# The head of a hybrid mLSTM / differential-attention layer: first modulation weights, then tokens, then the rest

## The chip, the cores and the metric

The kernel runs on one core of one Trainium2 chip. The metric is the device time of one execution in microseconds (us); of the kernel before, three timed executions are shown (median 2418.31 us, 2416.95 to 2418.4), and one more was profiled. The engines are named as in the profile: PE is TensorE (PEld its weight loads), DVE VectorE, ACT ScalarE, POOL GpSimd, SP SyncE, which issues DMAs.

## What is computed

One layer over 256 latent tokens `x` and 256 context tokens `ctx`, 2048 channels, all in float32. Only the beginning matters here:

```python
mod = jax.nn.silu(c) @ w_mod[l] + b_mod[l]            # sh1, sc1, ... for latent tokens
mod_c = jax.nn.silu(c_ctx) @ w_mod[l] + b_mod[l]      # csh1, csc1, ... for context tokens
h = modulate(rmsnorm(x, norm1_w[l]), sh1, sc1)
hc = modulate(rmsnorm(ctx, norm1_w[l]), csh1, csc1)
y, yc = token_mixer(h, hc, ...)                       # begins with h @ w_in and hc @ w_in
```

Then come the mLSTM and attention branches, the merge, and an expert retrieval (PEER).

## The kernel before, in words

The stretch around the change is called the head here: everything in `build` from line 308 to `drain()` on line 439. It makes the modulated, transposed tokens `hL` and `hC` (128 channels on the partitions, 16 chunks of channels) and, as they come, multiplies them with the first two blocks of `w_in` ("vm" and "zm").

**Modulation weights.** The main loop (line 408) goes over the 16 chunks k. Each chunk has four loads of 512 KB on SP's queue (line 417, through `load`, line 102) into a ring of 11 buffers. Every load is used by four matmuls (line 419), which the trace records as 8 each. The sums of a chunk stand in one PSUM tile `m`; `mod_evac` copies it (line 355), adds four partial sums with small matmuls (line 359) and writes shift and scale `mc` (lines 362, 364).

**Tokens.** `tokens()` loads four tiles of 128 tokens (1024 KB each, line 329), squares each on ACT for the norm (line 333), takes the power -1/2 on POOL (line 188), scales the tile on DVE (line 336), and turns it by 16 PE transposes in four groups (line 341), each group copied from a PSUM tile `m` back over the tile by ACT or DVE (line 343).

**h.** `h_chunk(k)` reads chunk k of all four turned tiles, applies shift and scale on ACT (line 377), rounds on DVE (line 381) and takes the remainder on POOL (line 382). A gate matmul (line 368) follows for each chunk. `vm_part` and `zm_part` are the products with `w_in` (line 264): a vm part has 24 matmuls of 512 columns, a zm part 12, and there are 8 of each. A `w_in` piece is loaded (line 104), rounded to `hi` on ACT (line 120) and its remainder `lo` made on DVE (line 123).

**Order.** The steps are generators in a queue `back`; `pump(n)`, called after each load of a chunk, runs n of them. So `pump` sets the order in the program. The order in which each engine then gets its instructions is made at build time by a list scheduler: it follows the program, but takes a later instruction whose inputs it believes to be ready when an engine would otherwise stand idle. At run time each engine goes through its list in that order.

**PSUM.** The pool of `m` tiles has four buffers. One is held by the gate sums `g_ps` through the head, two by `zm_acc` from the first zm part on; the sums of a chunk, their second step and the groups of transposes share what is left.

**POOL's queue** loads small tables at the start: the gate weights `gwp` (832 KB, line 322), `gbias`, `iota`, `bic` (lines 324 to 326) and two bias rows spread over all partitions (`brow`, 256 KB each, lines 346 and 347, through `row_to_all`, line 154). `crow` (line 411) is a small load that stands in the program at chunk 4.

Of the kernel before, what the change touches and what calls it, by code (L numbers as in the profile page):

```python
# [30 lines left out]
P = 128  # L31
# [42 lines left out]
def build(tc, a, dump=None):  # L74
    nc = tc.nc
# [18 lines left out]
    def col(shape, name, src=None, dt=F32):  # L94
        t = cst.tile(shape, dt, name=name)
        if src is not None:
            nc.gpsimd.dma_start(t, src)
        return t
# [3 lines left out]
    def load(src, pool, bufs, queue=nc.sync):  # L102
        r = pool.tile([P, 1024], F32, name="raw", tag="raw", bufs=bufs)
        d = queue.dma_start(r, src)  # L104
        if by_four[0]:
            tc.keep_in_program_order(d)
        return r
# [45 lines left out]
    def row_to_all(dst, src, n):  # L153
        nc.gpsimd.dma_start(dst, bass.AP(tensor=src.tensor, offset=src.offset, ap=[[0, P], [1, n]]))
# [6 lines left out]
    ident = col([P, P], "ident")  # L161
# [10 lines left out]
    iota = col([P, P], "iota")  # L172
    bic = col([P, 64], "bic")
# [10 lines left out]
    def rstd(pool, ss, n, w, name):  # L184
        v = pool.tile([P, w], F32, name=name + "v", bufs=1)
        nc.vector.tensor_scalar(v, ss, 1.0 / n, EPS, op0=OP.mult, op1=OP.add)
        r = pool.tile([P, w], F32, name=name, bufs=1)
        nc.gpsimd.tensor_tensor(r, v, mhalf[:, :w], op=OP.pow)  # L188
        return r
# [4 lines left out]
    def acc_tile():  # L194
        return psA.tile([P, 512], F32, name="acc", tag="acc")

    def m_tile():
        return psM.tile([P, 512], F32, name="m", tag="m")
# [7 lines left out]
    def brow_tile(row, blk):  # L206
        b = gco.tile([P, 512], F32, name="brow", tag="brow", bufs=2)
        row_to_all(b, a["b_in_rows"][row, blk * 512:(blk + 1) * 512], 512)
        return b
# [6 lines left out]
    def hT(s, c, k, tok=None):  # L216
        t = (hC if c else hL)[s][k // 4][:, k % 4]
        return t if tok is None else t[:, tok * P:(tok + 1) * P]
# [4 lines left out]
    back = []  # L223
# [6 lines left out]
    def step(q):  # L230
        while q:
            try:
                next(q[0])
                return
            except StopIteration:
                q.pop(0)

    def pump(rate, ahead=2, beside=0):
        for i, (q, r) in enumerate(((front, ahead), (back, rate), (side, beside))):
            credit[i] += r if q else 0  # L240
            while credit[i] > 0.99:
                credit[i] -= 1
                step(q)
# [75 lines left out]
    xt = [x4[:, i, :] for i in range(4)]  # L319
    sq = st.tile([P, D], mybir.dt.bfloat16, name="sq")  # L320
    gwp = st.tile([P, KT, 104], F32, name="gwp")
    nc.gpsimd.dma_start(gwp, a["w_gate"])
    gbias = cst.tile([104, 1], F32, name="gbias")
    nc.gpsimd.dma_start(gbias, a["gate_bias"])
    nc.gpsimd.dma_start(iota, a["iota"])
    nc.gpsimd.dma_start(bic, a["b_in_cols"])
    def tokens():
        for i in range(4):
            nc.sync.dma_start(xt[i], (a["x"] if i < 2 else a["ctx"])[(i % 2) * P:(i % 2 + 1) * P, :])
            yield  # L330
        for i in range(4):
            ss = st.tile([P, 1], F32, name=f"ss{i}")
            nc.scalar.activation(sq, xt[i], AF.Square, accum_out=ss)
            yield
            rs = rstd(st, ss, D, 1, f"rs{i}")
            nc.vector.tensor_scalar(xt[i], xt[i], rs, None, op0=OP.mult)
            yield
            for j in range(4):
                tp = m_tile()
                for k in range(4):  # L340
                    nc.tensor.transpose(tp[:, k * P:(k + 1) * P], xt[i][:, (4 * j + k) * P:(4 * j + k + 1) * P], ident)
                d = xt[i][:, j * 512:(j + 1) * 512]
                (nc.vector.tensor_copy if j % 2 else nc.scalar.copy)(d, tp)
                yield

    vm_brow = brow_tile(1, 0)
    zm_brow = brow_tile(2, 0)
    vm_acc = [acc_tile() for _ in range(4)]
    g_ps = m_tile()
    mod1 = {}  # L350
# [2 lines left out]
    def mod_evac(k, ps):  # L353
        r4 = st.tile([P, T], F32, name="r4", tag="r4", bufs=2)
        nc.vector.tensor_copy(r4, ps[:, 0:T])
        yield
        pc = m_tile()
        for s in range(2):
            mm(pc[:, 2 * s:2 * s + 2], lhsT=r4[:, s * P:(s + 1) * P], rhs=sel4, start=True, stop=True)
        m = mod1[k]  # L360
        for s in range(2):
            nc.vector.tensor_scalar(m[:, s, :], pc[:, 2 * s:2 * s + 2], b1c[:, s, k:k + 1], float(s),
                                    op0=OP.add, op1=OP.add)
        nc.vector.tensor_scalar(m[:, 1, :], m[:, 1, :], nwc[:, 0, k:k + 1], None, op0=OP.mult)
        yield

    def gate_part(k, hf):
        mm(g_ps[0:104, :], lhsT=gwp[:, k, :], rhs=hf, start=k == 0, stop=k == 15)
# [3 lines left out]
    def h_chunk(k):  # L372
        mc = mod1[k]
        hf = st.tile([P, 512], F32, name="hf", tag="hf", bufs=2)
        for c in range(2):
            w = slice(c * T, (c + 1) * T)
            nc.scalar.activation(hf[:, w].rearrange("p (i t) -> p i t", i=2), x4[:, 2 * c:2 * c + 2, k * P:(k + 1) * P],
                                 AF.Identity, bias=mc[:, 0, c:c + 1], scale=mc[:, 1, c:c + 1])
        for c in range(2):
            w = slice(c * T, (c + 1) * T)  # L380
            nc.vector.tensor_copy(hT(0, c, k), hf[:, w])
            nc.gpsimd.tensor_tensor(hT(1, c, k), hf[:, w], hT(0, c, k).bitcast(F32), op=OP.subtract)
        hfs.append(hf)
        yield
        if k:
            gate_part(k - 1, hfs[k - 1])
        if k == KT - 1:
            yield
            gate_part(k, hf)
        yield  # L390
# [3 lines left out]
    def first_part(j):  # L394
        (vm_part, zm_part)[j % 2](j // 2)
# [4 lines left out]
    def zm_part(kp):  # L400
        if kp == 0:
            zm_acc.extend(m_tile() for _ in range(2))
        token_part(zm_acc, take(), kp, h_lhs, kp == 0, kp == 7)

    back.append(tokens())
    part = 0
    ready = [0]
    for k in range(KT):
        if k == 4:
            crow = st.tile([KT, P], F32, name="crow")  # L410
            nc.gpsimd.dma_start(crow, a["c_row"])
            nc.scalar.activation(crow, crow, AF.Silu)
            nc.gpsimd.dma_start(s_dram.rearrange("o (k p) -> (o k) p", p=P), crow)
        mod1[k] = st.tile([P, 2, 2], F32, name="mc", tag="mc", bufs=4)
        ps = m_tile()
        for kp in range(4):
            w = load(a["w_mod1"][k, kp], stx, MOD_BUFS)
            for k4 in range(4):
                mm(ps[32 * k4:32 * k4 + 32, 0:T], lhsT=s1[:, 4 * kp + k4, :], rhs=w[:, k4 * T:(k4 + 1) * T],
                   start=kp == 0, stop=kp == 3, skip_group_check=True)  # L420
            pump(2 if k < 6 else 1)
            if kp % 2:
                if part // 2 * 2 + 1 < ready[0]:
                    first_part(part)
                    part += 1
                ready[0] = len(hfs)
        g = mod_evac(k, ps)
        next(g)
        front.append(g)
        back.append(h_chunk(k))  # L430
        look[0] = 2
    while part < 16:
        while part // 2 * 2 + 1 >= len(hfs):
# [1273 lines left out]
```

## Time and profile before

| what | value |
|---|---|
| median of three timed executions | 2418.31 us |
| the profiled execution's own time | 2422.88 us |
| its span, first to last instruction | 2421.2 us |
| PE busy over the span | 2326.2 us (96%) |
| DVE, ACT, POOL busy | 64%, 47%, 37% |
| read from HBM | 524.33 MB |
| first matmul of the head | 6.46 us |
| first matmul with `w_in` | 40.06 us |

The busy shares are means over stages with different limits. For a change in the first 40 us of 2421 the views by stretch and by order of time are the ones to read.

### The profile page before, as it was taken

Reading aid. Unit: us, or ns where it says so; the run is one execution under the profiler, and the core shown is the slowest. Engines: PE = TensorE matmul, PEld = TensorE weight load, DVE = VectorE, ACT = ScalarE, POOL = GpSimd, SP = SyncE. Lnnn points to the kernel's source line nnn. Section 1 sums busy time; section 2 is a strip of 40 time slices with the busy share of each in tenths; the row PEclk is TensorE's granted clock in tenths of the full one; section 3 lists DMA queues with packets and bytes.
Section 4 is the critical chain, followed back from the end, with each engine's and each line's share of the span. In section 5 each row is a group of like instructions: output and inputs, shape, how many; then the busy total and the mean of one; then the engine's idle time right before and its main releaser. Section 6 shows DMA issues by size and latency. Waiting matters only on the chain. (4 is left out here: it accounts for less than half of the span.)

```text
span 2421.2 us, 38180 instructions
## 1 busy us (share of the span) xinstructions
PE 2326.2 (96%) x14434; PEld 1971.9 (81%) x14434; DVE 1542.8 (64%) x2808; ACT 1140.5 (47%) x1913; POOL 894.1 (37%) x910
## 2 busy tenths in 40 slices
PE   6999999999999999989999989999999998999996
PEld 3679989998898999779888878887889887665663
DVE  3357874669766768564788976675665545444445
ACT  3231322244548544444446766794358643333333
POOL 2132201236533200000145564672237524656552
PEclk9999999999999999999999999999999999999998
DMA  9969855875536788755565567788765568998884
GB/s 383 347 201 321 318 192 180 287 214 165 153 115 189 239 281 272 244 197 184 165 200 173 174 183 222 218 219 238 216 191 170 163 213 293 385 368 321 344 337 158
DMA packets 235899, 571.04 MB, mean 236 GB/s; under 512 B 85138, under 2 KB 118723, under 8 KB 221248
## 3 DMA queue, kind: packets, MB, share of 16 engines
q1 hardware_dynamic: 153744, 338.29, 43.7%
q0 software_dynamic: 47120, 212.72, 24.7%
q10 hardware_dynamic: 34848, 17.57, 2.5%
q8 instruction: 113, 1.85, 0.3%
q14 instruction: 74, 0.61, 0.1%
HBM read 524.33 MB, written 38.93 MB: 233 GB/s over the span
## 5 line engine op out<-in xcount | busy, mean ns | idle before, releaser
L120 ACT CAST hi<-raw 128x1024 fp32r<-128x1024 f32 x528 | 552.4, 1048 | 794.0 <-PE acc L275 257.3
L123 DVE TENSOR_TENSOR lo<-raw,hi 128x1024 fp32r<-128x1024 f32 x465 | 590.2, 1272 | 328.8 <-ACT hi L120 323.0
L80 PE MATMUL s<-h,hi 128*128 128x512 f32 x2048 | 740.4, 403 | 1.0 <-ACT hi L120 1.0
L80 PE MATMUL s<-h,lo 128*128 128x256 f32 x2048 | 579.5, 283 | 20.8 <-POOL lo L123 11.5
L80 PEld LDWEIGHTS s<-h,hi 128*128 128x128 f32 x2048 | 388.2, 190 | 88.7 <-ACT hi L120 1.7
L275 PE MATMUL acc<-hL,hi 128*128 128x256 f32 x2048 | 420.5, 285 | 0.0
L80 PEld LDWEIGHTS s<-h,lo 128*128 128x128 f32 x2048 | 390.0, 190 | 28.7 <-POOL lo L123 14.2
L275 PEld LDWEIGHTS acc<-hL,hi 128*128 128x128 f32 x2048 | 339.4, 192 | 4.2 <-issue 3.9
L275 PE MATMUL acc<-hL,lo 128*128 128x256 f32 x1024 | 291.3, 285 | 3.9 <-DVE lo L123 3.9
L123 POOL TENSOR_TENSOR lo<-raw,hi 128x1024 fp32r<-128x1024 f32 x63 | 152.4, 2419 | 275.5 <-ACT hi L120 261.7
L1525 PE MATMUL v<-hi,l 128*128 128x512 f32 x704 | 197.7, 398 | 8.7 <-ACT l L1450 8.6
L1444 DVE TENSOR_TENSOR lo<-vraw,hi 128x1024 fp32r<-128x1024 f32 x106 | 129.2, 1234 | 118.1 <-ACT hi L1442 116.3
L275 PEld LDWEIGHTS acc<-hL,lo 128*128 128x128 f32 x1024 | 196.2, 192 | 5.9 <-DVE lo L123 4.9
L104 POOL DMA_DIRECT2D raw<-w_mod x128 | 67.9, 531 | 305.9 <-DVE raw L508 284.7
L508 DVE SCALAR_TENSOR_TENSOR raw<-raw,cr 128x1024 f32<-128x1024 f32 x128 | 154.9, 1221 | 36.9 <-DMA raw<-w_mod 21.4
L1223 POOL TENSOR_SCALAR o<-iota,i1T,gT 128x128 f32<-128x128 f32 x128 | 140.8, 1107 | 94.5 <-PE g L80 50.3
L1442 ACT CAST hi<-vraw 128x1024 fp32r<-128x1024 f32 x106 | 108.7, 1046 | 138.4 <-PE v L1525 134.0
L1525 PEld LDWEIGHTS v<-hi,l 128*128 128x128 f32 x704 | 132.5, 190 | 49.5 <-issue 10.6
L1429 POOL DMA_INDIRECT vraw<-expert_v,idxV x99 | 105.7, 1068 | 105.4 <-DVE l L1451 31.5
L275 PE MATMUL acc<-hC,hi 128*128 128x256 f32 x512 | 134.0, 283 | 0.0
L1507 DVE TENSOR_REDUCE act<-s 128x256 f32<-128x512 f32 x126 | 86.4, 686 | 58.1 <-PE s L80 52.8
L1429 POOL DMA_INDIRECT ag<-ag_dram,idxG x99 | 102.6, 1036 | 47.3 <-issue 26.2
(406 smaller groups left out, 3971.9 us busy)
## 6 DMA issues: line engine op xcount, KB each, us to landing
raw<-expert_u SPq DMA_DIRECT2D x256, 512.0 KB, 4.1
raw<-w_in SPq DMA_DIRECT2D x176, 512.0 KB, 4.5
raw<-w_mod POOLq DMA_DIRECT2D x128, 512.0 KB, 5.3
raw<-w_mod SPq DMA_DIRECT2D x64, 512.0 KB, 7.4
raw<-w_out SPq DMA_DIRECT2D x32, 512.0 KB, 3.6
raw<-w_pq SPq DMA_DIRECT2D x32, 512.0 KB, 3.3
ag_dram<-gates SPq DMA_DIRECT2D x32, 512.0 KB, 6.7
ag_dram<-act ACTq DMA_DIRECT2D x126, 128.0 KB, 4.0
```

The costliest lines, as they stand in the source:

```text
L80: tc.keep_in_program_order(mm(*args, **kw))
L104: d = queue.dma_start(r, src)
L120: nc.scalar.copy(h, r)
L123: (nc.vector if shared[0] else nc.gpsimd).tensor_tensor(l, r, h.bitcast(F32), op=OP.subtract)
L275: mm(acc[c][:, g * T:(g + 1) * T], lhsT=hl[sb][:, k2 * 512 + c * P:k2 * 512 + (c + 1) * P], rhs=rhs(sa, g, k), start=first and k2 == 0 and ...
L508: product = nc.vector.scalar_tensor_tensor(r, r, 1.0, cr, op0=OP.mult, op1=OP.mult, accum_out=part[:, h, i:i + 1])
L1223: (nc.gpsimd if i % 2 else nc.vector).tensor_scalar(o2[:, i, 0:width], iota[:, 0:width], cols[:, i:i + 1], factor[:, i:i + 1], op0=OP.is_e ...
L1429: tc.keep_in_program_order(nc.gpsimd.indirect_dma_start(out=out, out_offset=None, in_=src, in_offset=bass.IndirectOffsetOnAxis(ap=idx[:, b ...
L1442: nc.scalar.copy(h, raw)
L1444: nc.vector.tensor_tensor(l, raw, h.bitcast(F32), op=OP.subtract)
L1507: nc.vector.reduce_sum(act[:, e], ps.rearrange("p s t -> p t s"), axis=AX.X)
L1525: mm(out_acc[t][hf_ * 2 + c], lhsT=ins[sa], rhs=hl[sb][:, c * 512:(c + 1) * 512], start=first and i == 0, stop=last and i == 2, skip_group ...
```

## The change

The order of loads on SP becomes: the four loads of chunk 0, then all four token tiles, then chunk 1 and on. In `tokens()` the transposes are no longer done tile by tile; after all four tiles are scaled, `quarter(0)` turns channels 0 to 511 of the four tiles, and `quarter(1)` to `quarter(3)` are put into `back` after chunks 1, 5 and 9. Whether ACT or DVE copies a group now goes by the tile, not by the quarter. `pump` runs nothing after the first three loads of chunk 0, and four steps after its last load and after each load of chunk 1. The load of `gwp` stands at chunk 1 of the program, those of `brow`, `gbias`, `iota` and `bic` at chunk 4.

```diff
-    nc.gpsimd.dma_start(gwp, a["w_gate"])
     gbias = cst.tile([104, 1], F32, name="gbias")
-    nc.gpsimd.dma_start(gbias, a["gate_bias"])
-    nc.gpsimd.dma_start(iota, a["iota"])
-    nc.gpsimd.dma_start(bic, a["b_in_cols"])
...
             nc.vector.tensor_scalar(xt[i], xt[i], rs, None, op0=OP.mult)
             yield
-            for j in range(4):
-                tp = m_tile()
-                for k in range(4):
-                    nc.tensor.transpose(tp[:, k * P:(k + 1) * P], xt[i][:, (4 * j + k) * P:(4 * j + k + 1) * P], ident)
-                d = xt[i][:, j * 512:(j + 1) * 512]
-                (nc.vector.tensor_copy if j % 2 else nc.scalar.copy)(d, tp)
-                yield
-
-    vm_brow = brow_tile(1, 0)
-    zm_brow = brow_tile(2, 0)
+        yield from quarter(0)
+
+    def quarter(j):
+        for i in range(4):
+            tp = m_tile()
+            for k in range(4):
+                nc.tensor.transpose(tp[:, k * P:(k + 1) * P], xt[i][:, (4 * j + k) * P:(4 * j + k + 1) * P], ident)
+            d = xt[i][:, j * 512:(j + 1) * 512]
+            (nc.vector.tensor_copy if i % 2 else nc.scalar.copy)(d, tp)
+            yield
+
...
     for k in range(KT):
+        if k == 1:
+            nc.gpsimd.dma_start(gwp, a["w_gate"])
         if k == 4:
+            vm_brow = brow_tile(1, 0)
+            zm_brow = brow_tile(2, 0)
+            nc.gpsimd.dma_start(gbias, a["gate_bias"])
+            nc.gpsimd.dma_start(iota, a["iota"])
+            nc.gpsimd.dma_start(bic, a["b_in_cols"])
             crow = st.tile([KT, P], F32, name="crow")
...
-            pump(2 if k < 6 else 1)
+            pump((0 if kp < 3 else 4) if k == 0 else 4 if k == 1 else 2 if k < 6 else 1)
...
         back.append(h_chunk(k))
+        if k % 4 == 1 and k < 12:
+            back.append(quarter(k // 4 + 1))
```

## Rows read from the trace of the kernel before

**Rows 1.** The page, part 2: PE in 40 equal slices of the span, busy tenths.

```profile
PE   6999999999999999989999989999999998999996
```

**Rows 2.** Windows: length, busy us of PE, PEld, DVE, ACT, POOL, then clock, DMA share, GB/s.

```profile
20.00:40.00 20.00, 16.04 (x128) 8.61 (x128) 8.85 (x20) 8.57 (x13) 2.55 (x4) 0.74 1.02 410
...
140.00:160.00 20.00, 18.27 (x99) 12.90 (x98) 6.53 (x19) 5.17 (x8) 8.41 (x17) 0.91 0.31 95
...
160.00:600.00 440.00, 437.20 (x3047) 406.91 (x3046) 321.52 (x518) 141.48 (x201) 120.21 (x180) 1.00 0.74 243
```

**Rows 3.** Waits of PE up to 40 us, then from 40 to 160: total, times, longest.

```profile
PE m L419 <- DMA raw<-w_mod: 19.5, 5, 8.2
...
PE m L368 <- ACT hf L377: 1.7, 1, 1.7
```

**Rows 4.** Timeline of PE, 0 to 41 us: start, length, count, idle before.

```profile
6.46 1.08 PE L419 MATMUL m<-raw,s 128*32 128x256 f32 x8 [6.46 <-DMA raw<-w_mod]
...
15.71 1.08 PE L419 MATMUL m<-raw,s 128*32 128x256 f32 x8 [8.17 <-DMA raw<-w_mod]
...
23.14 1.08 PE L419 MATMUL m<-raw,s 128*32 128x256 f32 x8 [4.45 <-DMA raw<-w_mod]
...
24.44 1.08 PE L419 MATMUL m<-raw,s 128*32 128x256 f32 x8 [0.22 <-DMA raw<-w_mod]
...
31.55 1.08 PE L419 MATMUL m<-raw,s 128*32 128x256 f32 x8
...
33.21 0.64 PE L419 MATMUL m<-raw,s 128*32 128x256 f32 x8
...
36.91 1.53 PE L341 MATMUL m<-ident,x 128*128 128x128 f32 x12
...
40.06 0.73 PE L264 MATMUL acc<-hi,hL 128*128 128x512 f32 x2 [0.46 <-ACT hi L120]
```

**Rows 5.** Timeline of ACT and DVE: the token tiles' steps.

```profile
9.13 1.91 ACT L333 ACTIVATE sq<-x 128x2048 bf16<-128x2048 f32 x1 [6.33 <-DMA x<-x]
...
11.99 1.29 DVE L336 TENSOR_SCALAR x<-x,rs 128x2048 f32<-128x2048 f32 x1 [0.68 <-POOL rs L188]
...
19.59 1.91 ACT L333 ACTIVATE sq<-x 128x2048 bf16<-128x2048 f32 x1 [1.12 <-DMA x<-ctx]
...
21.92 1.91 ACT L333 ACTIVATE sq<-x 128x2048 bf16<-128x2048 f32 x1 [0.33 <-DMA x<-ctx]
```

**Rows 6.** Timeline of the queues SP and POOL and of DVE, 0 to 30 us.

```profile
1.63 0.27 DVE L567 MEMSET mrow<- 40x256 f32 x1
...
3.21 0.55 POOL L322 DMA_DIRECT2D gwp<-w_gate  x1
...
4.96 19.84 SPq L104 DMA_DIRECT2D raw<-w_mod  x10
5.43 1.08 POOL L154 DMA_DIRECT2D brow<-b_in_rows  x2
...
8.24 0.52 POOL L411 DMA_DIRECT2D crow<-c_row  x1 [1.73 <-DMA nwc<-norm_cols]
...
25.69 2.88 SPq L104 DMA_DIRECT2D raw<-w_in  x3
```

**Rows 7.** DMA issues up to 45 us: count, KB each, median us to landing.

```profile
raw<-w_in SPq DMA_DIRECT2D x4, 512.0 KB, 10.2
gwp<-w_gate POOLq DMA_DIRECT2D x1, 832.0 KB, 10.3
brow<-b_in_rows POOLq DMA_DIRECT2D x2, 256.0 KB, 12.3
```

**Rows 8.** PSUM tiles m: DVE's copies (ns min/median/max), first zm matmul, a later chunk.

```profile
L343 DVE COPY x<-m x8: 678/692/693, 18.7 to 48.2; 128x512 f32<-128x512 f32 x8
...
59.19 0.50 PE L264 MATMUL m<-hi,hL 128*128 128x512 f32 x1
...
73.86 1.93 PE L419 MATMUL m<-raw,s 128*32 128x256 f32 x32 [0.44 <-DVE mc L362]
```

## The prediction

> **What bounds the kernel now.** I read the page's slices first: PE is busy nine tenths or more of nearly every slice, the first excepted, where it is six [rows 1]. So time is to be had only where PE stands still or runs slow, and for this change that is the head. The windows say the same: from 160 to 600 us PE is busy 437.2 of 440 us [rows 2], so PE time saved in the head should come through one to one. The waits of PE come next: up to 40 us it waits 19.5 us in five pieces for modulation weights; from there to 160 us only for a few short things, 1.7 us at the end of the head among them [rows 3]. The timeline tells where the 19.5 us lie: 6.46 us before anything is there, 8.17 us before the second load of chunk 0, 4.45 us before the third, then two of 0.2 us [rows 4]. After 24.4 us PE has work without a break (56 more transposes and the weights as they land). One more loss shows there: a group of eight matmuls takes 1.08 us at 31.55 and 0.64 us at 33.21 [rows 4], and the granted clock from 20 to 40 us is 0.74 [rows 2]. So PE ran at 1.2 GHz until about 32.6 us, some 9.5 us after it took up steady work at 23.14.
>
> DMA is the other side of it: 410 GB/s from 20 to 40 us [rows 2], and loads of SP land in the order of issue, one 512 KB load every 1.3 us (23.14 to 24.44) [rows 4]. The change alters that order and none of the bytes.
>
> **The change, part by part. Loads on SP.** It moves four issues (1024 KB each) behind three weight issues. Before, 3072 KB had landed by 15.71 (two loads, two tiles), 4096 KB by 19.59 (first context tile), 5120 KB by 21.9 and 6144 KB by 24.44 (fourth load) [rows 4, 5]. The same bytes in the new order are four loads by about 11 us, and the token tiles at about 15.7, 19.6, 21.9 and 24.4. So the last tile comes some 2.5 us later than before, and everything from chunk 1 on keeps its place: chunk 1 lands from 25.7 on. The first `w_in` piece also keeps its place if it still follows twelve weight loads: issued at 25.69, landed 10.2 us later, 35.9 [rows 6, 7]. Issue time on SP costs nothing: its queue is eight loads ahead of the landings (ten issues take 19.84 us, since they wait for landings [rows 6]).
>
> **What PE gains.** From landing to scaled tile it takes 4.15 us (9.13 to 11.99 + 1.29 [rows 5]), so the tiles are ready for transposing at 19.9, 23.8, 26.1 and 28.6. Before, at 23.14, PE had done two loads and eight transposes: 2 x 0.48 + 8 x 0.128 = 2.0 us at full clock (1.93 us for the four loads of a chunk [rows 8]; 1.53 us for twelve transposes [rows 4]). After, at 19.9, it has done all four loads of chunk 0: 1.9 us. The same state is reached 3.2 us earlier. If PE has work without a break from there, and the clock rises as long after as it did before, 3.2 us are saved; the two waits of 0.2 us go too, and those before the first part, 0.46 us and another like it for `lo`, since the loads of chunk 2 and the gate matmuls can stand there: **4.8 us is the upper end.** The lower end: only the groups of quarter 0 are there before chunk 1 lands. Then at 25.7 PE has done 1.9 + 8 x 0.128 = 2.9 us of work against 2.0 + 2.6/2 = 3.3 before, and if the clock rises 9.5 us after that, at 35.2 and not 32.6, half of 2.6 us is lost too. That is 1.7 us lost, less the 1.2 us of waits that go: **0.5 us slower.** Which end is nearer depends on whether groups of the later quarters move up into the wait for tokens. The rows speak for it: the scheduler put the memset of line 567, which stands after the head, at 1.63 us and the load of `crow`, from chunk 4, at 8.24 us [rows 6]; a scaled tile's transposes are as ready. Against it: a group needs a PSUM tile, at half clock some 1.0 us on PE and then a copy, 0.69 us on DVE [rows 8], and ACT has a square of 1.91 us for every tile in the same stretch [rows 5], with the even tiles' copies queued behind it. I take two thirds of the upper end, 3.2 us.
>
> **Quarters and PSUM.** The transposes, copies and squares are the same in number. With h of chunks 0 and 1 ready earlier, the first zm part (59.19 us before [rows 8]) comes some 16 us earlier, two chunks, and from there one PSUM tile is left for sums, second steps and groups. In that state PE waits 0.44 us for the second step before a chunk's sums [rows 8]: 2 x 0.44 = 0.9 us lost. A full collision would cost more (a rival, below), none at all 0.
>
> **Loads on POOL.** They are taken out of the start in the program, but POOL has nothing else to do there: `gwp` goes out at 3.21 us right after the small tables, and `crow`, from the very place the others are moved to, went out before the first token had come [rows 6]. So I count no change of traffic; the other bound is in the rivals. Cover if they do wait: `gwp` lands 10.3 us after its issue [rows 7], 20 us before a gate matmul can want it; bias rows, `gbias`, `iota` and `bic` are used only after the head.
>
> **pump.** More steps per load up to chunk 1 and the parts one chunk earlier move PE work, none is added: 0.
>
> **Sum.** 3.2 - 0.9 = 2.3 us less: the span goes from 2421.2 to 2418.9 us, the profiled execution from 2422.88 to 2420.6. That execution lies 4.6 us (0.19%) above the median; from the median, 2418.31 - 2.3 = **2416.0 us**. What a measurement of this kernel can tell from no change is about 0.2%, 4.8 us.
>
> On the clock: the matmuls at 6.46, 15.71 and 23.14 us, each after a wait, all took 1.08 us [rows 4], half the later rate. The Trainium skill (TensorE: Matmul & The Clock Gate, Part 1) says that an idle PE has its clock gated to half and only activity releases it; the trace agrees. It speaks against this change: chunk 0 is done early and PE then waits for tokens, so the clock would start low whatever came before. By that rule with nothing moved up, the sum is the lower end; with transposes moved up, the upper.
>
> **Rivals.**
> *The wait is not filled (0.21).* The scheduler leaves the quarters where the program has them, PE stands until 25.7 and the clock rises late: 0.5 us lost, and 0.9 us for PSUM: 2419.7 us. For it: three free PSUM tiles and the squares on ACT; against it: the two instructions moved up [rows 6].
>
> *POOL's loads do leave the start (0.08).* Then the tokens have the DMA engines for themselves. `gwp` and the two bias rows, 832 + 2 x 256 KB or 1.38 MB [rows 7], are 3.4 us at 410 GB/s: tiles 3.4 us earlier, 2.3 + 3.4 = 5.7 us saved, 2412.6 us. Against it: `crow` at 8.24 [rows 6]. The Trainium skill (DMA: Bandwidth & Descriptors, Queues, rings and completion order) has each DMA engine take turns between the queues with work; the third tile's 3.9 us for 1024 KB (15.7 to 19.6), against 2.6 at 1.3 us per 512 KB, agrees.
>
> *The end of the head closes up (0.13).* PE waits 1.7 us there for the last h chunks [rows 3], and the clock is 0.91 from 140 to 160 us [rows 2], 0.09 x 20 = 1.8 us more. If the last chunks come ahead by the order made anew, that is 3.5 us on top of 2.3: 2412.5 us. Nothing in the diff aims at it.
>
> *Slower: groups collide in the last PSUM tile (0.12).* Quarters 2 and 3 stand in the program after chunks 5 and 9, where `zm_acc` and `g_ps` hold three of four tiles. If their eight groups are left there, each keeps the next chunk's sums waiting for its copy, 0.69 us and the 0.44 us seen at such a change of hands [rows 8]: 8 x 1.13 = 9.0 us, less 2.3: 2425.0 us. It turns the sign from three such groups on, and passes 0.2% from seven. Against it: the many products of line 264 that can stand between.
>
> **How the numbers follow.** The forecast has 0.46. Its own range is 0.5 us slower with 0.9 us for PSUM to 4.8 us faster with none: 2413.5 to 2419.7. The range for 8 in 10 takes in the two faster rivals and the unfilled wait and leaves the slower one out: 2411.0 to 2421.0. Faster by over 0.2%: 0.08 + 0.13 and 0.04 of the forecast's upper end, 0.25. Slower by over 0.2%: 0.12 and 0.01 for what the order made anew may do elsewhere, 0.13. Within: 0.62.
>
> **What would show it.** Right: four groups of line 419 done before 13 us; a first square at about 15.7 us and the last near 24.4 us; transposes of several quarters between 20 and 26 us; 0.64 us groups by about 30 us; the first vm product near 37 us and not 40.06; PE's waits for weights about 3 us shorter; zm near 43 us. Wrong: squares at 12 us (POOL's loads have moved); PE still at 1.08 us per group after 33 us; transposes at 60 to 100 us with waits of line 419 for line 343. The prediction fails as a whole if time changes after 160 us, where I count no change.

## The result, and the profile after

The changed kernel takes 2431.59 us (median of five runs, 2429.07 to 2433.41); the kernel before took 2418.4 beside it (five runs, 2416.95 to 2420.15). The ratio is 1.0054, with a 95% interval of 1.0039 to 1.0069: **slower by 13.2 us**, where 2416.0 was forecast and 2421.0 was the upper end of the range. The profiled execution took 2433.31 us with a span of 2431.6, which is 10.4 more than the span of before.

The page's slices of PE look almost the same as [rows 1]; a slice is 61 us long, and what is lost per slice is too little for a digit:

```profile
PE   6889999999999999999999989999999998999996
```

The waits of PE say where to look. First view: up to 40 us; second: 40 to 180 us (total, times, longest):

```profile
PE m L425 <- DMA raw<-w_mod: 21.6, 5, 11.5
...
PE m L358 <- DVE r L354: 5.2, 7, 1.6
PE acc L264 <- DVE hL L380: 2.6, 4, 0.7
PE m L425 <- DVE mc L361: 1.8, 4, 0.4
PE m L342 <- DVE mc L361: 1.3, 3, 0.4
PE m L367 <- ACT hf L376: 1.0, 2, 0.6
PE m L425 <- DVE x L344: 0.8, 1, 0.8
PE m L358 <- DVE mc L361: 0.8, 1, 0.8
```

The matmuls of the chunk sums are now line 425 (419 before), the transposes line 342 (341), their copies 344 (343), the second step 358 (359), the copies before and after it 354 and 361 (355 and 362), the gate matmuls 367 (368). Two readings. The wait for weights did not shrink from 19.5 us [rows 3], it grew to 21.6, and 11.5 of that is one wait. And where before had 3.8 us of short waits from 40 to 160 us (1.7 at the end of the head [rows 3], 0.9 for `mc`, 1.2 for `hi` and `lo`), there are now 13.7 us up to 180. Nearly all are for copies out of PSUM tiles `m` (354, 361, 344), 9.9 us together, or for `hL`, the end of the chain behind them, 2.6 us.

The timeline of PE shows both (start, length, count, idle before):

```profile
25.95 1.08 PE L425 MATMUL m<-raw,s 128*32 128x256 f32 x8 [11.48 <-DMA raw<-w_mod]
...
27.84 1.95 PE L342 MATMUL m<-ident,x 128*128 128x128 f32 x8
...
32.63 2.03 PE L425 MATMUL m<-raw,s 128*32 128x256 f32 x24
...
41.00 0.71 PE L264 MATMUL acc<-hi,hL 128*128 128x512 f32 x2
...
48.78 0.50 PE L264 MATMUL m<-hi,hL 128*128 128x512 f32 x1
...
117.78 0.60 PE L342 MATMUL m<-ident,x 128*128 128x128 f32 x4
...
118.45 0.40 PE L264 MATMUL acc<-lo,hL 128*128 128x512 f32 x1
...
123.24 0.60 PE L342 MATMUL m<-ident,x 128*128 128x128 f32 x4
124.63 1.93 PE L425 MATMUL m<-raw,s 128*32 128x256 f32 x32 [0.78 <-DVE x L344]
127.23 0.61 PE L358 MATMUL m<-sel,r 128*128 128x2 f32 x4 [0.67 <-DVE r L354]
128.27 0.66 PE L342 MATMUL m<-ident,x 128*128 128x128 f32 x4 [0.44 <-DVE mc L361]
129.56 0.80 PE L264 MATMUL acc<-hi,hL 128*128 128x512 f32 x1 [0.63 <-DVE hL L380]
130.15 0.63 PE L264 MATMUL acc<-lo,hL 128*128 128x512 f32 x1
```

From 14.47 to 25.95 PE stands: its list has the first group of chunk 1 ahead of any transpose, so no transpose runs, although the first token tile was squared from 17.0 on and scaled by 21.1 (line 334). The first vm product comes at 41.00 (40.06 before [rows 4]), the first zm product at 48.78 (59.19 before [rows 8]). Then, from 123.24 to 129.56, one PSUM tile is handed round: a group of transposes, its copy (wait 0.78), the sums of a chunk, their copy (0.67), the second step, its copy (0.44), the next group, and then even the products of line 264 have no `h` to work on (0.63). Before, the transposes were over at 48 us (the copies of line 343, [rows 8]). Now the groups of quarters 2 and 3 start at 78.58, 83.60, 90.09, 96.69, 117.78, 123.24, 128.27 and 134.75 us.

The sums tell the same by their beat. Before, the last group of a chunk came every 7.5 us (106.2, 113.6, 121.2, 128.7, 136.2, 143.6 us); after, at 100.2, 103.7, 111.2, 126.2, 138.2, 141.8 and 149.3.

The windows add what a wait does not show (same columns as [rows 2]):

```profile
80.00:100.00 20.00, 17.35 (x116) 11.69 (x120) 7.74 (x12) 4.95 (x7) 2.83 (x4) 0.91 0.49 193
...
120.00:140.00 20.00, 16.69 (x118) 11.01 (x116) 6.23 (x13) 3.56 (x5) 1.46 (x2) 0.91 0.49 184
```

The granted clock is 0.91 in three stretches of 20 us (the third, from 160 to 180, answers to the one of before at 140 to 160 [rows 2]). Two more than before would be 2 x 0.09 x 20 = 3.6 us. The rows of the timeline give the price more directly: single products of line 264 take 0.63 us from 92.1 and from 130.2 us on, where 0.39 to 0.40 is usual (118.45). How much was waited and how much was slow work is told by the window from the start to the first matmul of line 275, the first behind the head; the kernel before, then the kernel after:

```profile
0.00:208.00 208.00, 184.71 (x1160) 126.25 (x1161) 102.56 (x214) 64.99 (x86) 50.04 (x83) 0.97 0.86 313
...
0.00:222.90 222.90, 187.44 (x1161) 129.22 (x1162) 105.79 (x217) 65.15 (x86) 47.77 (x84) 0.98 0.78 292
```

PE is idle for 23.3 us before and 35.5 after, 12.2 more: some 2.4 of them up to 40 us (21.6 and 0.3 for a copy, against 19.5) and 13.7 - 3.8 = 9.9 behind that. It is busy 2.7 us longer with all but the same number of recorded matmuls. That is mainly the slower clock: there are twelve such slow products, and each takes 0.2 us more. The line views of the first matmuls behind the head (line 275 in both) and of the last part of the kernel (line 1525, now 1533) show how late PE really is; first the kernel before:

```profile
L275 PE MATMUL acc<-hL,hi x2048: 277/283/469, 208.0 to 877.2; 128*128 128x256 f32 x187
...
L1525 PE MATMUL v<-hi,l x704: 387/393/795, 2031.3 to 2401.9; 128*128 128x512 f32 x176
```

and the kernel after:

```profile
L275 PE MATMUL acc<-hL,hi x2048: 277/283/472, 222.9 to 892.5; 128*128 128x256 f32 x187
...
L1533 PE MATMUL v<-hi,l x704: 387/393/792, 2041.6 to 2412.2; 128*128 128x512 f32 x176
```

14.9 us late at 208, 15.3 at 877, 10.3 at 2031 and at 2402. So the whole loss is made in the head; 4.6 us of it come back after 1200 us in this pair of executions, where before has the lower clock (0.97 from 1400 to 1600 us, after 0.98). That pair is not the rule: the medians are 13.2 apart, and the profiled execution of before lies 4.5 us above its median, that of after 1.7.

Loads went nearly as forecast. The squares, which follow the landings of the token tiles, and POOL's issue of `gwp`:

```profile
16.98 1.91 ACT L331 ACTIVATE sq<-x 128x2048 bf16<-128x2048 f32 x1 [14.13 <-DMA x<-x]
...
24.71 1.91 ACT L331 ACTIVATE sq<-x 128x2048 bf16<-128x2048 f32 x1 [0.49 <-DMA x<-ctx]
...
3.22 0.55 POOL L409 DMA_DIRECT2D gwp<-w_gate  x1
```

### The profile page after: what moved, and what is told of

The parts are those of the page before. It is cut to its first block, busy times and chain, and to the rows that moved or that the text cites. A ratio compares the mean times of both kernels' runs of the same rounds, so it can differ in the third digit from the quotient of the medians.

```text
span 2431.6 us, 38184 instructions
## 1 busy us (share of the span) xinstructions
PE 2324.3 (96%) x14434; PEld 1971.0 (81%) x14434; DVE 1542.7 (63%) x2808; ACT 1139.8 (47%) x1913; POOL 889.3 (37%) x910
## 5 line engine op out<-in xcount | busy, mean ns | idle before, releaser
L80 PE MATMUL s<-h,lo 128*128 128x256 f32 x2048 | 578.2, 282 | 20.0 <-DVE lo L123 10.3
L516 DVE SCALAR_TENSOR_TENSOR raw<-raw,cr 128x1024 f32<-128x1024 f32 x128 | 154.7, 1219 | 40.3 <-DMA raw<-w_mod 21.9
L1450 ACT CAST hi<-vraw 128x1024 fp32r<-128x1024 f32 x106 | 108.6, 1046 | 138.5 <-PE v L1533 134.1
L275 PE MATMUL acc<-hC,hi 128*128 128x256 f32 x512 | 134.1, 283 | 0.0
```

Of the source, the lines that this page charges most:

```text
L80: tc.keep_in_program_order(mm(*args, **kw))
L275: mm(acc[c][:, g * T:(g + 1) * T], lhsT=hl[sb][:, k2 * 512 + c * P:k2 * 512 + (c + 1) * P], rhs=rhs(sa, g, k), start=first and k2 == 0 and ...
L516: product = nc.vector.scalar_tensor_tensor(r, r, 1.0, cr, op0=OP.mult, op1=OP.mult, accum_out=part[:, h, i:i + 1])
L1450: nc.scalar.copy(h, raw)
```

## The experiments

The theory to be tested: **quarters 2 and 3 come so late that they share the last PSUM tile with sums and second steps, and that turn-taking makes the loss.** Rivals: the load order (PE stands 11.5 us), the moved POOL loads, and the late data itself (`h` of a late chunk waits for its turned tokens). Each kernel is compared with runs of the kernel before on the same chip, whose median stands beside it where it changes; "waits" are the sums of PE's waits for 40 to 180 us, "late" is the start of line 275 (276 where a kernel has one line more) less 208.0. Where idle and busy time of PE are given, they are those up to that start.

### One part at a time

**Load order and pump alone**, with the transposes tile by tile as before:

```diff
-        yield from quarter(0)
+            for j in range(4):
+                tp = m_tile()
...
-        if k % 4 == 1 and k < 12:
-            back.append(quarter(k // 4 + 1))
```

> Loads and pump of the changed kernel, but each token tile is transposed whole as soon as it is scaled, as before the change; no quarters. Theory A (the eight groups of quarters 2 and 3, done from 78 to 135 us, take turns with the chunks' sums in the one PSUM tile that is left): all transposes are over before the first zm product, the waits of PE from 40 to 180 us fall from 13.7 us to under 5, and the time is 2416 to 2420 us. Theory B (the order of loads: PE waits for tokens and starts slow): still about 2431 us, with the waits up to 40 us near 21.6 us. Theory C (the scheduler's order made anew is worse by itself, whichever edit caused it): anything from 2420 to 2431.

2424.04 us against 2418.13, ratio 1.0022 (1.001 to 1.0035): slower, by 6 us. Waits 7.0 us, late 4.0. The first vm product comes only at 46.1 us, since all sixteen groups (28.4 to 42.6 us) stand between the loads and `h`. So the load order without the quarters is no gain, and it is not the bulk of the 13 us either. The time lies above the range of theory A, though no group is late.

**Quarters alone**, in the kernel before:

```diff
+        yield from quarter(0)
...
+        if k % 4 == 1 and k < 12:
+            back.append(quarter(k // 4 + 1))
```

> The kernel before with the quarters alone: loads, POOL's loads and pump as before. Theory A: eight groups come late here too, so 2428 to 2433 us, with PE waits for a second step or a copy in the stretch from 60 to 140 us. Theory B: as before, 2418 us. Theory C: anything between.

2432.65 us, ratio 1.0062 (1.0042 to 1.0083): 14.5 us slower, as much as the whole change. Waits 13.5, late 11.6; groups of quarters 2 and 3 at 76.9 to 131.5. Its waits from 40 to 180 us are the list of after, total by total, but for the last one of 0.2; the three longest (line numbers differ):

```profile
PE m L362 <- DVE r L358: 5.2, 7, 1.6
PE acc L264 <- DVE hL L384: 2.6, 4, 0.7
PE m L422 <- DVE mc L365: 1.8, 4, 0.4
```

**Quarters early**: everything of the change, but quarters 1 to 3 queued together after chunk 1:

```diff
-        if k % 4 == 1 and k < 12:
-            back.append(quarter(k // 4 + 1))
+        if k == 1:
+            back.extend(quarter(j) for j in range(1, 4))
```

> The changed kernel with quarters 1 to 3 put into the queue together, right after chunk 1, so that their twelve groups stand ahead of most of the chunks. Theory A: they are done before or soon after the zm sums take their two PSUM tiles, and most of the 13 us goes: 2416 to 2422 us. Theory B: 2431 us, since loads are as in the changed kernel. Theory C: anything between.

2416.4 us, ratio 0.9998 (0.9985 to 1.0011): the loss is gone. The waits from 40 to 180 us, and the line of the transposes, which now end at 59.8 us, after zm has begun at 55.0:

```profile
PE m L367 <- ACT hf L376: 1.7, 1, 1.7
PE m L425 <- DVE x L344: 0.8, 1, 0.8
PE m L342 <- ACT x L344: 0.7, 1, 0.7
PE m L425 <- DVE mc L361: 0.4, 1, 0.4
...
L342 PE MATMUL m<-ident,x x64: 270/273/476, 27.9 to 59.8; 128*128 128x128 f32 x64
```

13.7 us of waits have become 3.6; the 1.7 at the end of the head is there as in [rows 3]. The beat of 7.5 us is back from chunk 5 on. The 11.5 us wait for weights is there in this kernel too, so that wait is not what costs.

**POOL's loads back** at the start of the program:

```diff
+    nc.gpsimd.dma_start(gwp, a["w_gate"])
     gbias = cst.tile([104, 1], F32, name="gbias")
+    nc.gpsimd.dma_start(gbias, a["gate_bias"])
...
+    vm_brow = brow_tile(1, 0)
+    zm_brow = brow_tile(2, 0)
```

> The changed kernel with the gate weights, bias rows, gbias, iota and bic issued at the start of the program again. Theory A and theory B: no difference to the changed kernel, 2429 to 2434 us, because POOL issued them in its first 8 us anyway. Theory D (POOL's loads in their new place cost time): back toward 2418 us.

2433.29 us, ratio 1.0063 (1.0044 to 1.0082), waits 13.4: as slow as after. So no cost of that part of the change can be told from these runs.

### Data or tile?

**Idle groups**: quarters early, and eight more groups where quarters 2 and 3 stood. They turn tokens again and copy them where nobody reads them, so no data is late:

```diff
+    def idle_groups(j):
...
+            d = sq.bitcast(F32)[:, (i % 2) * 512:(i % 2 + 1) * 512]
...
+        if k in (5, 9):
+            back.append(idle_groups(k // 4 + 1))
```

> e3_quarters_early with eight more groups of four transposes, put into the queue after chunks 5 and 9 where quarters 2 and 3 stand in the changed kernel. They take a PSUM tile m each and are copied by ACT and DVE into a buffer that nobody reads, so no h chunk needs them. They add 8 x 4 x 0.128 = 4.1 us of PE work. Theory A (turns in the one PSUM tile that is left): the cost of the changed kernel comes back on top of that work, 2428 to 2435 us. Rival E (h chunks wait for late transposes, the data, not the tile): only the 4.1 us of work, 2419 to 2422 us.

2428.16 us against 2414.95, ratio 1.0064 (1.0047 to 1.008): 13.2 us slower. The groups run at 80.5 to 134.1, late is 14.0, and the waits are 11.8 us in all:

```profile
PE m L367 <- DVE r L363: 3.1, 5, 0.8
PE acc L264 <- DVE hL L389: 2.4, 4, 0.7
PE m L434 <- DVE mc L370: 1.3, 3, 0.4
```

Eight groups add 8 x 0.6 = 4.8 us of PE work by the 0.60 us of a group; the waits are 8.2 us longer than with the quarters early (11.8 and 3.6). In the change the eight groups add no work, only waits, 10.1 us more than with the quarters early (13.7 and 3.6). Groups that give nothing to anybody bring 8.2 of these 10.1, so late data can be a small part at most.

**zm late**: the change as it is, but five vm parts before the first zm part, so that the two tiles of `zm_acc` are taken only behind the last group. The order of the `w_in` loads goes with it (0 is vm, 1 is zm):

```diff
+SEQ = [(0, 0), (0, 1), (0, 2), (0, 3), (0, 4), (1, 0), (1, 1), (0, 5), (1, 2), (1, 3), (0, 6), (1, 4), (1, 5), (0, 7),
+       (1, 6), (1, 7)]
...
-        (vm_part, zm_part)[j % 2](j // 2)
+        (vm_part, zm_part)[SEQ[j][0]](SEQ[j][1])
```

> The changed kernel, quarters late as they are, but the first five vm parts ahead of the first zm part (the pieces of w_in loaded in that order), so that the two PSUM tiles of the zm sums are taken only after the last quarter is due. The work is the same. Theory A: three tiles are free while quarters 2 and 3 are turned, so 2416 to 2423 us; waits of PE for a second step, a copy or mc between 60 and 140 us under 5 us. Rival E: 2428 to 2433 us.

2418.39 us, ratio 1.0019 (1.0003 to 1.0036). The late groups are still late (70.4 to 108.4 us), but with three tiles free for them the waits on tiles are gone; the list of 40 to 180 us is down to 4.1:

```profile
PE m L368 <- ACT hf L377: 3.6, 4, 1.3
PE m L359 <- DVE r L355: 0.3, 1, 0.3
```

The longest entry of after, 5.2 us of the second step for the copy of its sums, is a wait for data, and it too is down to 0.3: with more tiles free, other matmuls stand in the list between the two. It is 3.5 us late, and those are lost before 40 us: PE is busy 16.61 us there against 20.10 in the kernel before.

**The controls for zm late.** The same edit in the kernel before:

> The kernel before with the first five vm parts ahead of the first zm part, as in e6_zm_late, and nothing else. The control for e6_zm_late, e10 and e12. Theory A: before, the one-tile stretch costs PE only 0.9 us of waits, so little is to be had: 2413 to 2419 us. If the order of parts is worth something by itself (zm parts left over for the end of the head, where PE waits 1.7 us and the clock falls), 2413 us; if late zm parts leave PE short of work in the middle, over 2420.

2423.59 us against 2417.41, ratio 1.0024 (1.0011 to 1.0036), so zm late by itself costs 6 us, with waits of 5.6, more than the 2413 to 2419 us that were expected. The changed kernel with zm late (above) lies 3.4 us over the kernel before: once zm is late, the rest of the change, late groups and all, costs nothing more. With the early quarters:

> e3_quarters_early with zm late. Theory A: that run's waits for tiles (3.6 us from 40 to 180 us) go, the rest stays: 2413 to 2418 us. Theory C (the list's order decides, the tile does not): anything up to 2428.

2421.83 us, ratio 1.0013 (0.9997 to 1.0028), waits 4.6: no gain on the early quarters without it, and above the expected 2413 to 2418 us. The early quarters had few waits for the tile left to take away (3.6 us in all), and zm late costs something by itself.

### Can the wait be filled?

**Two tiles first**: the latent tiles are turned whole, ahead of chunk 1, and the rest as the early quarters:

```diff
+            if i < 2:
+                for j in range(4):
+                    yield from group(i, j)
...
-            pump((0 if kp < 3 else 4) if k == 0 else 4 if k == 1 else 2 if k < 6 else 1)
+            pump((0 if kp < 3 else 16) if k == 0 else 4 if k == 1 else 2 if k < 6 else 1)
```

> The fill that the prediction counted on, made by hand: the loads of the changed kernel, the two latent tiles transposed whole as soon as they are scaled and ahead of chunk 1 in the queue, of the context tiles quarter 0 first and the other quarters right after chunk 1. PE works from about 21 us and not 26. Theory A with the prediction's working: 2 to 5 us less than e3_quarters_early, 2412 to 2415 us. Theory B (the clock is low there anyway, and PE gains nothing from work before 26 us): no better than e3_quarters_early, 2416 us or more.

2420.17 us, ratio 1.0034 (1.0014 to 1.0054). PE does take transposes into the wait now (from 21.6 us), but the waits from 40 to 180 us are 7.8 us: zm starts at 50.7, and the beat of 7.5 us is lost without any late group. So the fill brings no gain here, as theory B had it. With zm late as well:

> e7_two_tiles_first with zm late. That run began 2 us ahead at the 16th chunk load and lost it again to waits for tiles (7.8 us from 40 to 180 us). Theory A: those go, 2412 to 2417 us, the best of all kernels here. Theory C: anything up to 2428.

2420.28 us, ratio 1.0015 (0.9998 to 1.0032), waits 5.5. No clear gain, and not the 2412 to 2417 us that were expected.

**Early quarters with the loads of before** (the edit of quarters early, in the kernel before):

> Quarters early as in e3_quarters_early, but loads, POOL and pump of the kernel before: it differs from e3_quarters_early by the order of loads alone. If the order of loads is worth something by itself (my sum: 0 to 3 us), 2416 to 2420 us; if it costs (e1_by_tile, with the same loads, lies 6 us above before), 2411 to 2415 us.

2427.44 us, ratio 1.0052 (1.0031 to 1.0073): a miss for the simple form of the theory. All groups are done by 61 us, zm starts at 52.8, and yet waits are 10.2 us, and the clock 0.91 from 60 to 100 us. With zm late:

> e8_early_old_loads (2427 us, all transposes done by 61 us, and still 10 us of waits from 40 to 180 us) with zm late. Theory A (its waits are turns in the one tile, which its last four groups met just after the zm sums had taken two): 2414 to 2420 us. Rival F (the old order of loads does not go with quarters, whatever the tiles): still about 2427 us.

2420.84 us, ratio 1.0011 (1.0 to 1.0023), and the waits on tiles are nearly gone. First the early quarters with the loads of before, two of its eight lines:

```profile
PE m L422 <- DVE mc L365: 2.9, 5, 0.8
PE m L362 <- DVE r L358: 2.3, 3, 0.8
```

then the same with zm late, its two longest:

```profile
PE acc L265 <- DVE hL L385: 2.5, 3, 1.1
PE m L372 <- ACT hf L381: 1.7, 2, 1.5
```

So the tile is at work there too, but a late group is not needed: waits for the tile come as well from an order of the list in which sums, second steps and copies of successive chunks follow each other closely. What makes the scheduler take one order or the other stays open, and zm late changes the order as well as the free tiles; in the kernel before that cost 6 us.

### One turn less

If turns in one tile are the cost, a chunk should need fewer of them. Here the second step writes into spare columns of the tile that holds the sums, instead of taking a tile of its own:

```diff
-        pc = m_tile()
+        pc = ps[:, T:T + 4]
```

In the kernel after:

> The changed kernel with the second step of a chunk written into free columns of the PSUM tile that holds its sums, so that a chunk takes the one tile that is left once and not twice. Theory A1 (each time the tile changes hands costs, so fewer turns help): 2418 to 2426 us, and fewer than 10 us of waits from 40 to 180 us. Theory A2 (it is how long the tile is held: sums and second step now hold it through, and the groups wait longer): 2430 us or more.

2424.11 us against 2417.86, ratio 1.0026 (1.0012 to 1.0039): about half of the loss is gone, with the groups as late as ever. Waits 11.8, late 7.6. But the waits did not fall under 10 us as expected. Of the 7.3 us that line 275 starts earlier than in the kernel after, 2.2 are less idle time and 5.1 less busy time for the same matmuls (182.3 and 187.4 us), with full speed earlier (groups of eight take 0.64 us from 29.41 on): most of it is clock, and the price of a turn is not shown by this run. With the early quarters:

> e3_quarters_early with the same shared tile. A1: the waits for r and for the next tile (2 us) go, 2412 to 2417 us. A2: no less than e3_quarters_early, 2416 us or more.

2416.53 us, ratio 0.9995 (0.9985 to 1.0005): nothing to be had, where few waits for the tile were left. In the kernel before:

> The kernel before with the same shared tile, the control. It has no late groups and its second step already stands well behind its sums. A1 and A2: within 3 us of before, 2415 to 2421 us.

2414.97 us, ratio 0.9986 (0.9976 to 0.9997): 2.9 us faster, 5.9 early behind the head, and 1.4 early at 876 us. In that pair of executions the 5.9 us are not waits: idle time is 0.3 us less, busy time 5.6 less for the same matmuls (179.1 and 184.7), with a granted clock of 1.00 and not 0.74 from 20 to 40 us. And with two tiles first:

> e7_two_tiles_first with the same shared tile. A1: its 7.8 us of waits from 40 to 180 us fall under 4, 2411 to 2416 us. A2: 2418 us or more.

**2405.95 us (2404.45 to 2409.03), ratio 0.9954 (0.9938 to 0.997): 11.9 us faster than the kernel before, the fastest version here,** and faster than the 2411 to 2416 us that were expected. Its waits from 40 to 180 us, and PE in the wait for weights:

```profile
PE m L434 <- PE m L367: 2.4, 5, 0.5
PE m L376 <- ACT hf L385: 1.2, 3, 0.5
...
21.22 5.83 PE L351 MATMUL m<-ident,x 128*128 128x128 f32 x32 [5.06 <-DVE x L334]
26.98 0.64 PE L434 MATMUL m<-raw,s 128*32 128x256 f32 x8
29.95 0.63 PE L351 MATMUL m<-ident,x 128*128 128x128 f32 x4 [2.33 <-DVE x L334]
30.51 0.64 PE L434 MATMUL m<-raw,s 128*32 128x256 f32 x8
32.31 0.99 PE L351 MATMUL m<-ident,x 128*128 128x128 f32 x4 [1.16 <-DVE x L334]
```

Thirty-two transposes stand in the wait, and the waits behind 40 us are 3.6 us where two tiles first without the shared tile had 7.8. Line 275 starts 7.5 us earlier than there (203.2 and 210.7), 5.8 of them less idle time: here the shared tile did take waits away. It starts 4.8 us ahead of the kernel before, but that lead does not last. At the last of these matmuls, which began at 877.2 before, 0.9 is left:

```profile
L275 PE MATMUL acc<-hL,hi x2048: 277/283/472, 203.2 to 876.3; 128*128 128x256 f32 x187
```

In this pair of executions, 18.5 us apart, the lead is 2.4 us at 1168 us (first product of line 80), 11.4 at 2022 (the last) and 18.5 at the end. So most of the 11.9 us between the medians is not won in the head. From 1168 us on PE's wait for the remainders `lo` made on POOL is 6.1 us and not 11.5 (for those made on DVE it is 11.5 and not 9.2), and the clock from 1400 to 1600 us is 0.99 and not 0.97. What brings that was not tried; this part is measured, not explained.

Nor is a gain of the fill by itself shown. With the same loads and the shared tile but no fill, the early quarters are 1.4 us ahead of the kernel before at line 275, so the fill's version is 3.4 ahead of them; but the kernel before with the shared tile and no fill is 5.9 ahead.

## Why the prediction was wrong

**What bounds the kernel: right for a loss.** The loss is idle or slow PE in the head, and it came through almost one to one: 14.9 us late at 208 us, 15.3 at 877. Gains did not last so well: 5.9 and 4.8 us ahead behind the head were 1.4 and 0.9 at 876 (the two fastest versions with the shared tile). That no time changes after 160 us held until 1200; the 4.6 us that come back later in the profiled pair were not foreseen.

**Loads: right in the main.** The tiles were to land at about 15.7, 19.6, 21.9 and 24.4 us; their squares began at 16.98, 19.85, 22.21 and 24.71. The fourth load of chunk 0 came at 13.39 and not by about 11, and the first tile was scaled at 21.1 and not at 19.9, which alone takes 1.2 us from the 3.2 that the fill was to save. Chunk 1 was to land from 25.7 on; its first group ran at 25.95. POOL's loads counted at nothing: `gwp` left at 3.22 us (3.21 [rows 6]), and putting them back changed nothing that can be told.

**The fill of the wait, 3.2 us: wrong.** The step that failed is "a scaled tile's transposes are as ready": two instructions that had moved up, a memset on DVE and a load on POOL [rows 6], were taken as a sign of what the list of PE would do. The list of PE put no transpose ahead of the first group of chunk 1. The lower end, 0.5 us slower, was the right one: the first vm product came 0.9 us later. Written into the program (two tiles first, with the shared tile) the transposes do stand in the wait; even so the first vm product came at 42.00 and not near 37.

**The clock: a term that was mis-sized, and without weight.** A rise some 9.5 us after steady work begins was carried over from before. After, steady work began at 25.95, and the 24 matmuls from 32.63 took 2.03 us, where 24 take 1.50 at full speed (at 60.46), so it rose among them, between 6.7 and 8.7 us after. The rule of the Trainium skill that the prediction set beside it (TensorE: Matmul & The Clock Gate, Part 1: an idle PE has its clock halved, and only activity releases it) gave the lower end with nothing moved up, and that is how the start came out; the trace agrees, with 1.08 us for the group behind the wait of 11.48.

**PSUM sharing, 0.9 us: the step that decided.** The prediction saw that the early zm start leaves one tile for sums, second steps and groups, and then priced two chunks of that by [rows 8], 2 x 0.44. It had the collision as the slower rival (0.12, 2425.0 us), and its sign of being wrong, transposes at 60 to 100 us with waits of the sums for copies, is what the trace shows. Against that rival it held "the many products of line 264 that can stand between". They do so only in part: they need `h` of the chunks that the tile holds up, and wait for it themselves (2.6 us for `hL`).

**The rival's price was too low as well.** It had 8 x 1.13 = 9.0 us, where the waits from 40 us on grew by 9.9 (1.24 for each group, if all of it is put down to them). What it left out is the clock, 2.7 us of slower work, and the longer wait at the start, 2.4 us, and it still took off the gain that did not come. The median that the prediction started from, 2418.31, with 2.4 for the start, 9.9 for the waits and 2.7 for the clock is 2433.3, beside 2431.59 measured.

**The end of the head** did not close up: PE waits 2.2 us from 163 to 167 us, for the copies of the last chunk and its `hL`, where it waited 1.7 for `hf`, and the window at 0.91 is still there, 20 us later.

## What to carry to other kernels

Before steps are spread over a longer stretch, count for each PSUM tile how many users take it in turn in that stretch, and give a price to the whole round (write, copy, next write), not to one wait; here each of the eight late groups, 0.6 us of PE work, cost 1.8 us more on average (14.5 us for eight, in the quarters alone) once it had to share the last tile. Whether a scheduler fills a wait is read from the list of the engine in question, not from what it did on another; where the fill matters, write it into the program. If a turn can't be moved, taking one away is worth a try: two small results in one tile cost a line, and no version here became slower by it. The kernel before gained 2.9 us, the changed one some 7, the one with two tiles first went from 5.2 above the kernel before to 11.9 below. How much of that is the turn itself is open: in the head it was partly clock, and in the last case most was won far behind the head. So follow a gain through the whole kernel, not only to the end of the changed part.

## What was not expected of the hardware

The granted clock in the profile's rows does not show every slow stretch. In the kernel after, groups of eight matmuls took 1.08 us from 6 to 30 us and 0.64 us from 36.82 on, while the granted clock of 0 to 40 us is given as 1.00; in the kernel before it is 0.87 for the same stretch. The length of the groups is the surer sign.

How PE comes out of a wait differs. In the fastest version 32 transposes after a wait of 5.06 us took 5.83 us, and the next group was at 0.64 us already; four transposes after a wait of only 1.16 us then took 0.99 us, against 0.63 for the four before. In the kernel after, full speed was back between 32.63 and 34.66 us, after a wait of 11.48 us that ended at 25.95.

In the kernel after, the granted clock is 0.91 from 80 to 100 and from 120 to 140 us, where the longest single wait is 1.6 us, and twelve products there took 0.61 to 0.63 us each instead of 0.39 to 0.40; the kernel before has 1.00 in both. Many short waits on PE thus went with clock that was not given, besides the time waited.
